# The last gate columns and the output projection move into the ordered list of the MLP, with pairs by seven products and rings of five

## The chip, the cores and the metric

The kernel runs on one core of a Trainium2 chip. The metric is device time in microseconds (us), the median of several executions. TensorE (PE) does the matmuls, VectorE (DVE) and ScalarE (ACT) the elementwise work, the sync engine (SP) issues the loads.

## The reference

Two layers of a hybrid decoder on x of 1 x 256 x 2048, float32:

```
h = rms_norm(x, attn_norm)
g_q, g_k, g_v, g_gate, g_lr, s_q, s_k, s_v = split(h @ w_in)           # 6160 columns
o_gla = rms_norm(gla_chunked(g_q, g_k, g_v, log_a), gla_out_norm) * silu(g_gate)   # 1024 columns
o_sb  = rms_norm(stick_breaking_attention(rms_norm(s_q), rms_norm(s_k), s_v), sb_out_norm)
x = x + concat(o_gla, o_sb) @ w_o                                      # 2048 x 2048
hm = rms_norm(x, mlp_norm)
x = x + square(relu(hm @ w_up)) @ w_down                               # 2048 x 8192, 8192 x 2048
```

## The kernel before

Every matmul operand is split into a high part and a low rest: ScalarE copies a raw weight tile to `whi`, VectorE subtracts to get `wlo`, and each product is three matmuls (high by `whi`, high by `wlo`, low by `whi`), 128x512 each. A *piece* is one `whi` and one `wlo` tile of 1024 columns; mostly 12 matmuls read it.

**Up to the output projection** the work goes in units of 512 columns (`unit`, L537, weights by `weight_parts`, L512). A scheduler orders the engines; `after(n, fn)` (L341) holds other work until n ticks later. The last two input units (L1051) give the 1024 gate columns in two halves. Of each half ScalarE makes a scaled copy (L1056) and then absolute value, exponential and logarithm (L1058 to L1060), VectorE takes the minimum (L1061), ScalarE the exponential (L1062), VectorE the product (L1063). `gated` (L1040) multiplies the attention results `on` by it, and TensorE turns them into `mixed`, the operand of the output projection. That has four units of 512 columns (L1078), each followed by `residual` (L1074), one addition of 128x1024 into x (`xb`), and by `norm_operand`, which turns `xb` into the MLP's operand `hm`.

**The MLP** is an ordered list (`Plan`, L40) of entries with an engine, a length, what they need, and a due time counted back from TensorE's order. `Plan.run` (L68) walks through them, taking for VectorE and ScalarE what is due first of what is ready in its own reckoning; the order that comes out is kept on PE, DVE and ACT (L1448), behind all that was issued before. The list has units of 1024 columns: for each quarter q two up units and two down units. The contraction of a unit runs over eight *pairs* of 128-row blocks, each with a raw tile of 1 MB. Five pairs take 8 products of 128x512; pairs 1, 3 and 5 (`fast`, L398) take 7 by Strassen's scheme (in Winograd's form): VectorE then makes sums of the weights (`ts`, `t`, L1195 on) and of the operand (`forms`, L401), and the seven results gather in seven PSUM banks (`m1` to `m7`; `m8` takes part in the plain pairs). `down_tail` (L1266) and `up_tail` (L1313) put the banks together, with 12 additions of 128x512 after each unit. `whi` and `wlo` have four buffers each (`RING`), raw tiles five (`RAWS`). The list starts with four entries of TensorE that stand for the work still under way (L1111).

Of the kernel before, what the change touches and what calls it, by code (L numbers as in the profile page):

```python
# [126 lines left out]
def trunk_kernel(  # L127
# [61 lines left out]
    MLP = ("sxh", "sx", "ts", "t4", "raw2")  # L189
# [544 lines left out]
    def norm_pair(po):  # L734

        o = tmp("on", [P, 512], bufs=4)
# [39 lines left out]
    for l in range(DEPTH):  # L776
# [234 lines left out]
        def gla_out(e, v, vc, S, sc):  # L1011
# [21 lines left out]
            ons[e] = norm_pair(po)  # L1033
# [6 lines left out]
        def gated(e, gate, c):  # L1040
            o = ons[e]
            o4 = o.rearrange("p (h t d) -> p h t d", h=2, t=NT)
            for tt in range(NT):
                nc.vector.tensor_tensor(
                    o4[:, :, tt, :], o4[:, :, tt, :],
                    gate[:, tt, c : c + 2 * P].rearrange("p (h d) -> p h d", d=P), ALU.mult,
                )
            after(1, lambda: to_operand(mixed, e, o, gain("gla", l)))

        for g in range(2):  # L1050
            ug = unit(hT, wl, 0, C_GG + g * 512, 512)  # L1051
            gate = act_tile(F32, (P, NT, 512))

            def gate_part(tt, ug, gate):
                gx = gate[:, tt, :]
                nc.scalar.activation(gx, ug[:, tt, :], AF.Copy, scale=rst[:, tt : tt + 1])  # L1056
                e = tmp("t2", [P, 512], bufs=4)
                nc.scalar.activation(e, gx, AF.Abs)  # L1058
                nc.scalar.activation(e, e, AF.Exp, scale=-1.0)
                nc.scalar.activation(e, e, AF.Ln, bias=1.0)  # L1060
                nc.vector.scalar_tensor_tensor(e, gx, 0.0, e, ALU.min, ALU.subtract)  # L1061
                nc.scalar.activation(e, e, AF.Exp)  # L1062
                nc.vector.tensor_tensor(gx, gx, e, ALU.mult)  # L1063
# [24 lines left out]

        mlp_psum()
        hT = Operand()  # L1090
# [4 lines left out]
        RING, RAWS = 4, 5  # L1095
# [7 lines left out]
        units = [(q, down, n2) for q in range(4) for down in range(2) for n2 in range(2)]  # L1103
# [13 lines left out]
        def norm_last():  # L1117

            sq = add("ACT", 2 * A1, lambda: norm_squares(3, ssq), x3)
            return norm_end(sq, ssq)  # L1120
# [22 lines left out]
        def weights(u, j):  # L1143
            q, down, n2 = units[u]
            if down:
                r0, c0, w = q * 2048, n2 * 1024, w_down[l]
            else:
                r0, c0, w = 0, q * 2048 + n2 * 1024, w_up[l]
            r0 += 2 * j * P
            return w[r0 : r0 + 2 * P, c0 : c0 + 1024].rearrange("(k p) n -> p k n", p=P)  # L1150

        def load(x):
# [15 lines left out]
        def parts(src, readers, deps, n=2):  # L1168
# [3 lines left out]

            def high():
                box["h"] = ppool.tile([P, 2, 512], F32R, tag="whi", name=nm("whi"), bufs=RING)
                nc.scalar.activation(box["h"][:, :n], src(), AF.Copy)  # L1175

            def low():
                box["l"] = ppool.tile([P, 2, 512], F32R, tag="wlo", name=nm("wlo"), bufs=RING)
# [16 lines left out]
        def steps(x, r, ld, readers):  # L1195

            u, j = divmod(x, 8)
            q, down, n2 = units[u]
            op = up[q] if down else hm
# [290 lines left out]
```

## Time and profile before

| | us |
|---|---|
| median of 3 runs | 2199.61 (2199.44 to 2200.23) |
| the profiled execution | 2201.5 |
| its span | 2199.8 |
| TensorE busy | 2187.7 |
| VectorE busy | 1790.0 |
| ScalarE busy | 1259.7 |

TensorE is the engine that is nearly always busy. A busy span counts a matmul from its start to its modelled end, and neighbours overlap; the pace is read from one start to the next. "Idle before" in a row names what ended the wait.

### The profile page before, as it was taken

The page shows a single profiled execution, that of the slowest core. Times are in us where ns is not written, and L with a number is a line of the kernel's source. Part 1 is how long each engine was busy: PE and PEld are TensorE (multiplying, and loading weights), DVE is VectorE, ACT ScalarE, POOL GpSimd, SP SyncE. Part 2 cuts the span into 40 slices and gives each one's busy share as a digit, 9 for nine tenths or more (in the row PEclk, how much of TensorE's full clock was granted, in tenths as well). Part 3 has the DMA queues.
Part 4 walks back from the last instruction along what each step waited for, and adds up shares of the span by engine and source line. Part 5 has one row for each costly group of instructions (what it writes and reads, how often), then busy time and mean ns, then how long its engine had stood idle before and what let it go on. Part 6 is the DMA issues. An engine that isn't in the chain of part 4 may idle for free.

```text
span 2199.8 us, 27163 instructions
## 1 busy us (share of the span) xinstructions
PE 2187.7 (99%) x10376; PEld 1806.0 (82%) x10376; DVE 1790.0 (81%) x2286; ACT 1259.7 (57%) x1623; POOL 38.0 (2%) x64
## 2 busy tenths in 40 slices
PE   9999999999999999999999999999999999999999
PEld 7988778888888888888888887788888888888887
DVE  5677556789999999999957775667999899999998
ACT  5555345566566566466656553555665655665663
POOL 0020000000000000000000200000000000000000
PEclk9999999999999999999999999999999999999999
DMA  6654446556556556655546544465656665565564
GB/s 223 199 157 154 153 154 220 165 195 208 193 196 203 189 192 198 216 180 198 165 156 192 172 154 152 140 242 172 201 182 198 199 207 195 195 203 183 194 202 140
DMA packets 152550, 408.97 MB, mean 186 GB/s; under 512 B 6650, under 2 KB 31810, under 8 KB 152420
## 3 DMA queue, kind: packets, MB, share of 16 engines
q1 hardware_dynamic: 152420, 407.24, 56.3%
q8 instruction: 81, 1.33, 0.3%
q14 instruction: 49, 0.40, 0.1%
HBM read 405.12 MB, written 2.10 MB: 185 GB/s over the span
## 4 chain that ended last, share of the span: by engine, by line
PE 90%; DVE 7%; issue 1%; ACT 1%; DMA 0%; SPq 0%; POOL 0%; ACTq 0%
PE acc L549 9%; PE acc L551 9%; PE acc L550 9%; DVE wlo L1179 3%; PE acc L596 3%; PE acc L600 1%; DVE ts L1098 1%; DVE act L426 1%; PE ps L1017 1%; PE ps L1029 1%; ACT whi L1175 1%; PE ps L441 0%; PE ps L976 0%; PE ps L712 0%; DVE sx L426 0%
## 5 line engine op out<-in xcount | busy, mean ns | idle before, releaser
L1175 ACT ACTIVATE whi<-raw 128x1024 fp32r<-128x1024 f32 x512 | 532.5, 1057 | 280.4 <-DVE xb L1098 22.2
L1179 DVE TENSOR_TENSOR wlo<-raw,whi 128x1024 fp32r<-128x1024 f32 x512 | 618.5, 1217 | 56.8 <-ACT whi L1175 52.9
L532 DVE TENSOR_TENSOR wlo<-raw,whi 128x1024 fp32r<-128x1024 f32 (+2 forms) x274 | 317.3, 1164 | 194.3 <-ACT whi L530 193.8
L530 ACT ACTIVATE whi<-raw 128x1024 fp32r<-128x1024 f32 (+2 forms) x274 | 273.7, 1005 | 295.4 <-PE acc L551 246.9
L549 PE MATMUL acc<-whi,act 128*128 128x512 f32 (+2 forms) x960 | 368.9, 384 | 0.8 <-ACT act L451 0.8
L550 PE MATMUL acc<-wlo,act 128*128 128x512 f32 (+2 forms) x960 | 362.4, 377 | 0.0
L551 PE MATMUL acc<-whi,act 128*128 128x512 f32 (+2 forms) x960 | 362.2, 377 | 0.0
L549 PEld LDWEIGHTS acc<-whi,act 128*128 128x128 f32 x960 | 181.3, 189 | 35.9 <-issue 4.1
L551 PEld LDWEIGHTS acc<-whi,act 128*128 128x128 f32 x960 | 180.9, 188 | 34.1 <-issue 0.7
L550 PEld LDWEIGHTS acc<-wlo,act 128*128 128x128 f32 x960 | 181.3, 189 | 31.1 <-issue 0.7
L1175 ACT ACTIVATE whi<-ts 128x1024 fp32r<-128x1024 f32 x96 | 101.5, 1057 | 103.0 <-PE m__1438_7186 L1260 3.9
L1179 DVE TENSOR_TENSOR wlo<-ts,whi 128x1024 fp32r<-128x1024 f32 x96 | 117.3, 1222 | 51.6 <-ACT whi L1175 51.6
L1175 ACT ACTIVATE whi<-t 128x512 fp32r<-128x512 f32 x96 | 60.6, 631 | 122.2 <-DVE t L1098 60.7
L1098 DVE TENSOR_TENSOR ts<-raw 128x1024 f32<-128x1024 f32 x96 | 117.1, 1220 | 1.2
L596 PE MATMUL acc<-act,whi 128*128 128x512 f32 x256 | 91.9, 402 | 0.0
L600 PE MATMUL acc<-act,wlo 128*128 128x256 f32 x256 | 71.8, 280 | 0.0
L1179 DVE TENSOR_TENSOR wlo<-t,whi 128x512 fp32r<-128x512 f32 x96 | 65.5, 682 | 1.6 <-ACT whi L1175 1.5
L1098 DVE TENSOR_TENSOR raw<-ts,raw 128x512 f32<-128x512 f32 x96 | 65.5, 683 | 0.4
L1098 DVE TENSOR_TENSOR t<-raw 128x512 f32<-128x512 f32 x96 | 65.5, 682 | 0.0
L1344 ACT ACTIVATE act<-act,st 128x512 f32<-128x512 f32 x64 | 46.1, 720 | 26.3 <-DVE act L1098 25.4
L596 PEld LDWEIGHTS acc<-act,whi 128*128 128x128 f32 x256 | 48.1, 188 | 11.1
L600 PEld LDWEIGHTS acc<-act,wlo 128*128 128x128 f32 x256 | 48.4, 189 | 0.1
(2401 smaller groups left out, 4585.1 us busy)
## 6 DMA issues: line engine op xcount, KB each, us to landing
raw<-in_w_up_dram SPq DMA_DIRECT2D x128, 1024.0 KB, 5.1
raw<-in_w_down_dram SPq DMA_DIRECT2D x128, 1024.0 KB, 5.3
raw<-in_w_in_dram SPq DMA_DIRECT2D x84, 1024.0 KB, 5.1
raw<-in_w_o_dram SPq DMA_DIRECT2D x32, 1024.0 KB, 5.1
raw<-in_w_in_dram SPq DMA_DIRECT2D x14, 512.0 KB, 6.6
raw<-in_w_in_dram SPq DMA_DIRECT2D x8, 544.0 KB, 3.8
out_dram<-xb SPq DMA_DIRECT2D x8, 256.0 KB, 2.0
xb<-in_x_dram SPq DMA_DIRECT2D x3, 512.0 KB, 8.2
```

The lines of the kernel that those rows point to most:

```text
L426: nc.vector.tensor_tensor(d[:, :, 1, :], src, f32(d[:, :, 0, :]), ALU.subtract)
L530: newest["hi"] = nc.scalar.activation(h, r, AF.Copy).ins
L532: newest["lo"] = nc.vector.tensor_tensor(lo[:, q : q + step, :width], r, f32(h), ALU.subtract).ins
L549: nc.tensor.matmul(o, xh[:, sl], whi[:, j, :width], start=first, stop=False)
L550: nc.tensor.matmul(o, xh[:, sl], wlo[:, j, :width], start=False, stop=False)
L551: st["mm"] = nc.tensor.matmul(o, xl[:, sl], whi[:, j, :width], start=False, stop=last).ins
L596: nc.tensor.matmul(acc[:, f, :], whi[:, j, sl], op.both(k), start=(k == 0), stop=False, skip_group_check=True,)
L600: nc.tensor.matmul(acc[:, f, T:], wlo[:, j, sl], xh, start=False, stop=(k == KT - 1), skip_group_check=True,)
L1098: nc.vector.tensor_tensor(dst, a, b, op)
L1175: nc.scalar.activation(box["h"][:, :n], src(), AF.Copy)
L1179: nc.vector.tensor_tensor(box["l"][:, :n], src(), f32(box["h"][:, :n]), ALU.subtract)
L1344: nc.scalar.activation(box[h][:, tt, :], box[h][:, tt, :], AF.Relu, scale=rr[:, tt : tt + 1],)
```

## The change

The second half of the gate columns becomes the first unit ("g") of the ordered list, and the output projection its next two ("o"), with 1024 columns each. The gate's arithmetic becomes entries of the list (`gate`), for the first half as well, whose copies are still issued ahead of the list. In an o unit pairs 0 and 1 go by seven products, in the order given by `pair_order`, and the results are added to x by `down_tail`. `whi` and `wlo` get a fifth buffer (`whi5`, `wlo5`), raw tiles go from five to four. The attention's buffers give way to the MLP's (`open_scope`) before the second gate unit instead of after the first projection unit.

```diff
-    MLP = ("sxh", "sx", "ts", "t4", "raw2")
+    MLP = ("whi5", "wlo5", "sxh", "sx", "ts", "t4", "raw2")
...
+    def norm_pair(po, o=None):
+
+        o = tmp("on", [P, 512], bufs=4) if o is None else o
...
-            ons[e] = norm_pair(po)
+            if e % 2 == 0:
+                ons["t", e // 2] = act_tile(F32, (P, 2, 512))
+            ons[e] = norm_pair(po, ons["t", e // 2][:, e % 2, :])
...
-        def gated(e, gate, c):
-            o = ons[e]
...
-            after(1, lambda: to_operand(mixed, e, o, gain("gla", l)))
-
-        for g in range(2):
-            ug = unit(hT, wl, 0, C_GG + g * 512, 512)
-            gate = act_tile(F32, (P, NT, 512))
...
-            gate_part(0, ug, gate)
-            after(1, lambda a=ug, b=gate: gate_part(1, a, b))
-            for hp in range(2):
-                after(3 + hp, lambda e=2 * g + hp, t=gate, c=hp * 2 * P: gated(e, t, c))
...
+        ug = unit(hT, wl, 0, C_GG, 512)
+        gates_t = [act_tile(F32, (P, NT, 512))]
+        for tt in range(NT):
+            nc.scalar.activation(
+                gates_t[0][:, tt, :], ug[:, tt, :], AF.Copy, scale=rst[:, tt : tt + 1]
+            )
+        assert not held
...
+        open_scope("sbuf", mlp=1)
         hm = Operand()
         ssq = new_ssq()
...
-        def residual(n, acc):
-            nc.vector.tensor_tensor(xb[n], acc, xb[n], ALU.add)
-
-        for n in range(4):
-            uo = unit(mixed, w_o[l], 0, n * 512, 512, (2, 3, 0, 1))
-            if n == 0:
-
-                open_scope("sbuf", mlp=1)
-            if n < 3:
-                residual(n, uo)
-                after(1, lambda n=n: norm_operand(hm, n, "mlp", l, sums=True))
-                after(2, lambda n=n: norm_squares(n, ssq))
-        assert not held
-
-
...
-        RING, RAWS = 4, 5
+        RING, RAWS = 5, 4
...
-        units = [(q, down, n2) for q in range(4) for down in range(2) for n2 in range(2)]
+
+        units = [("g", 0, 0), ("o", 0, 0), ("o", 0, 1)]
+        units += [(k, q, n2) for q in range(4) for k in ("up", "down") for n2 in range(2)]
+
+        def pair_order(u):
+
+            if units[u][0] != "o":
+                return range(8), {j for j in range(8) if fast(j)}
+            if units[u][2] == 0:
+                return (4, 5, 6, 7, 0, 1, 2, 3), {0, 1}
+            return (4, 5, 6, 0, 7, 1, 2, 3), {0, 1}
...
-        tail = [add("PE", 12 * MM, None) for _ in range(RING)]
-        for t in tail:
-            whi.append([t])
-            wlo.append([t])
-        x3 = add("DVE", V2, lambda: residual(3, uo), tail)
...
+        for _ in range(RING):
+            p = add("PE", 12 * MM, None)
+            whi.append([p])
+            wlo.append([p])
...
-        def turned(n, h2, m, op, key, ll, deps):
-
-            turn, high, low, _ = operand_parts(op, n, h2, key, ll, lambda: bank(m))
-            a = add("PE", 8 * TR / 2, turn, deps, free.get(m))
...
+        def turned(n, h2, m, op, key, ll, sums=False):
+
+            turn, high, low, scaled = operand_parts(op, n, h2, key, ll, lambda: bank(m))
+            i = 2 * n + h2
+            a = add("PE", 4 * TR, turn, x_done[n], free[m])
+            if sums and fast(i):
+                box = []
+                b = add("ACT", A1, lambda: box.append(scaled()), a)
+                free[m] = [b]
+                return made(lambda: forms(op, i, box[0], "sxh"), None, True, b)
...
             box = []
+            x = len(raws)
 
             def fn():
-                if x % 5 < 2:
-                    box.append(tmp("raw2", [P, 2, 1024], bufs=2))
+                if x % 4 == 0:
+                    box.append(tmp("raw2", [P, 2, 1024], bufs=1))
                 else:
                     box.append(wpool.tile([P, 2, 1024], F32, tag="raw", name=nm("raw")))
-                nc.sync.dma_start(box[0], weights(*divmod(x, 8)))
...
+            def part(tag):
+                if i % RING == 0:
+                    return tmp(tag + "5", [P, 2, 512], F32R, bufs=1)
+                return ppool.tile([P, 2, 512], F32R, tag=tag, name=nm(tag), bufs=RING - 1)
+
             def high():
-                box["h"] = ppool.tile([P, 2, 512], F32R, tag="whi", name=nm("whi"), bufs=RING)
+                box["h"] = part("whi")
                 nc.scalar.activation(box["h"][:, :n], src(), AF.Copy)
...
+            kind, q, _ = units[u]
+            op = {"g": hT_now, "o": mixed, "up": hm, "down": up.get(q)}[kind]
...
+            if kind == "g":
+                for s in range(2):
+                    yield parts(
+                        lambda s=s: r()[:, s, :].rearrange("p (c n) -> p c n", c=2),
+                        readers, ld,
+                    ), [(m, [(blk(k, tt, 2 * j + s), k) for k in range(2)])
+                        for tt, m in enumerate((1, 6))]
+                return
...
-            if not fast(j):
+            if not is_fast:
...
+        def gate(g):
+
+            y = gates_t[g]
...
+                def logs(gx=gx, box=box):
+                    box.append(tmp("t2", [P, 512], bufs=4))
+                    nc.scalar.activation(box[0], gx(), AF.Abs)
+                    nc.scalar.activation(box[0], box[0], AF.Exp, scale=-1.0)
+                    nc.scalar.activation(box[0], box[0], AF.Ln, bias=1.0)
...
+                a = add("ACT", 3 * A1, logs, gate_done.get((g, tt)))
+                b = add("DVE", V1, least, a)
+                c = add(
+                    "ACT", A1,
+                    lambda box=box: nc.scalar.activation(box[0], box[0], AF.Exp), b,
+                )
+                ends.append(add("DVE", V1, lambda gx=gx, box=box: combine(gx(), gx(), box[0], ALU.mult), c))
...
+                a = add("DVE", 0.7, gated, ends)
+                turns.append((g, 4 * TR, turn, a, m, e, high, low, scaled, box))
+
+        def turn_gated():
+
+            g, cost, turn, a, m, e, high, low, scaled, box = turns.pop(0)
+            p = add("PE", cost, turn, a, free[m])
+            if e < 2:
+                b = add("ACT", A1, scaled, p)
+                free[m] = [b]
+                done["o", 0, e] = made(lambda: forms(mixed, e, box[1], "sx"), None, True, b)
+            else:
+                b = add("ACT", A1, high, p)
+                done["o", 0, e] = add("DVE", 0.7, low, b)
+                free[m] = [b, done["o", 0, e]]
+
...
+            for tt, m in enumerate((1, 6)):
+                free[m] = [gate_done.get((1, 0))]
+                gate_done[1, tt] = add("ACT", A1, lambda a=(tt, m): copy(*a), p[m], free[m])
+                free[m] = [gate_done[1, tt]]
+            gate(1)
...
-        lastf = max(j for j in range(8) if fast(j))
+        hT_now, hT = hT, Operand()
         rr = rr_done = None
...
+        gate_done, turns, tails = {}, [], {}
+        gate(0)
+        for u, (kind, q, n2) in enumerate(units):
+            order, quick = pair_order(u)
+            if kind != "g":
+                tails[u] = (up_tail if kind == "up" else down_tail)(u)
...
+            lasts = [j for j in order if j in quick][-1]
+            for j in range(4) if kind == "g" else order:
+                final = j == (3 if kind == "g" else order[-1])
+                r, ld, readers = load(u, j)
+                for (box, h, lo), prods in steps(u, j, j in quick, r, ld, readers):
...
-                    if u == 0 and k == 0:
+                    was = units[u - 1] if u else None
+                    if kind == "g" and k == 4 or kind == "o" and n2 == 0 and k == 5:
+                        turn_gated()
+                        turn_gated()
+                    if k < 2 and was and was[0] == "up":
+                        tails[u - 1][2](k)
+                    if k < 2 and was == ("o", 0, 0) or was == ("o", 0, 1) and k < 2:
+                        n = 2 * was[2] + k
                         for h2 in range(2):
-                            done["hm", 6 + h2] = turned(
-                                3, h2, (5, 7)[h2], hm, "mlp", l, x3
+                            done["up", 0, 2 * n + h2] = turned(
+                                n, h2, ((5, 7), (1, 6))[k][h2], hm, "mlp", l, sums=True
                             )
...
-                if j == lastf:
+                if j == lasts and kind != "g":
                     tails[u][0](p)
+            if kind == "g":
+                g_tail(p)
+            if kind == "o" and n2 == 1:
+                rr, rr_done = norm_end([squares(n, ssq) for n in range(4)], ssq)
```

What the built order makes of it is seen best where the first gate unit ends, in the first layer (the second has the same). ScalarE before: `whi` are the tiles of the second gate unit, `act_2724` the scaled copy of the first one's result, `t` the scratch of its logarithms.

```order
L530 ACTIVATE whi_2736<-raw_2734 128x1024
L530 ACTIVATE whi_2760<-raw_2734 128x1024
L737 ACTIVATE on_2672<-ps_2661 128x512
L364 ACTIVATE st_2679<-st_2678 128x4
L365 ACTIVATE st_2679<-st_2679 128x4
L530 ACTIVATE whi_2778<-raw_2776 128x1024
L1056 ACTIVATE act_2724<-acc_2487,st_444 128x512 x2
L1058 ACTIVATE t_507_2726<-act_2724 128x512
L1058 ACTIVATE t_512_2753<-act_2724 128x512
L1059 ACTIVATE t_507_2726<-t_507_2726 128x512
L1059 ACTIVATE t_512_2753<-t_512_2753 128x512
L1060 ACTIVATE t_507_2726<-t_507_2726 128x512
```

ScalarE now, at the same place: `act_2722` is the copy, `whi_534_2782` the first tile of the second gate unit.

```order
L365 ACTIVATE st_2677<-st_2677 128x4
L1045 ACTIVATE act_2722<-acc_2486,st_444 128x512 x2
L1418 ACTIVATE t_529_2758<-act_2722 128x512
L1419 ACTIVATE t_529_2758<-t_529_2758 128x512
L1420 ACTIVATE t_529_2758<-t_529_2758 128x512
L1418 ACTIVATE t_531_2764<-act_2722 128x512
L1419 ACTIVATE t_531_2764<-t_531_2764 128x512
L1420 ACTIVATE t_531_2764<-t_531_2764 128x512
L1431 ACTIVATE t_529_2758<-t_529_2758 128x512
L1431 ACTIVATE t_531_2764<-t_531_2764 128x512
L1183 ACTIVATE whi_534_2782<-raw_530_2762 128x1024
L1183 ACTIVATE whi_2784<-raw_530_2762 128x1024
```

Three `whi` tiles of the next unit stood ahead of the copy, and none does now; all of the first half's eight functions stand ahead of the first.

VectorE before, at the same place: `wlo` are the rests of the second gate unit's tiles.

```order
L532 TENSOR_TENSOR wlo_2737<-raw_2734,whi_2736 128x1024
L532 TENSOR_TENSOR wlo_2761<-raw_2734,whi_2760 128x1024
...
L532 TENSOR_TENSOR wlo_2779<-raw_2776,whi_2778 128x1024
L1061 SCALAR_TENSOR_TENSOR t_507_2726<-act_2724,t_507_2726 128x512
L1061 SCALAR_TENSOR_TENSOR t_512_2753<-act_2724,t_512_2753 128x512
L532 TENSOR_TENSOR wlo_2797<-raw_2776,whi_2796 128x1024
L1063 TENSOR_TENSOR act_2724<-act_2724,t_507_2726 128x512
L1063 TENSOR_TENSOR act_2724<-act_2724,t_512_2753 128x512
L1044 TENSOR_TENSOR on_2332<-on_2332,act_2724 128x2x128 x2
```

VectorE now, at the same place.

```order
L623 TENSOR_TENSOR act_2571<-act_2571,st_2680 128x512
L1423 SCALAR_TENSOR_TENSOR t_529_2758<-act_2722,t_529_2758 128x512
L1423 SCALAR_TENSOR_TENSOR t_531_2764<-act_2722,t_531_2764 128x512
L1063 TENSOR_TENSOR act_2722<-act_2722,t_529_2758 128x512
L1063 TENSOR_TENSOR act_2722<-act_2722,t_531_2764 128x512
L1441 TENSOR_TENSOR act_2332<-act_2332,act_2722 128x2x128 x4
L1187 TENSOR_TENSOR wlo_536_2786<-raw_530_2762,whi_534_2782 128x1024
L1187 TENSOR_TENSOR wlo_2790<-raw_530_2762,whi_2784 128x1024
```

The first `wlo` of the second gate unit now comes behind the minimum, the product and the four slices of the gating (L1441); three came ahead of them.

## Rows read from the trace of the kernel before

**Rows 1.** The page: busy time, share of the span and instructions of each engine.

```profile
PE 2187.7 (99%) x10376; PEld 1806.0 (82%) x10376; DVE 1790.0 (81%) x2286; ACT 1259.7 (57%) x1623; POOL 38.0 (2%) x64
```

**Rows 2.** TensorE in order of time (start, length), first layer's second up unit.

```profile
482.19 0.39 PE L1258 MATMUL m__784_4104<-whi,act 128*128 128x512 f32 x1
...
483.55 0.39 PE L1258 MATMUL m__756_3993<-whi,act 128*128 128x512 f32 x1
484.36 0.50 PE L1259 MATMUL m__756_3993<-wlo,act 128*128 128x512 f32 x1 [0.42 <-DVE wlo L1179]
```

**Rows 3.** TensorE's waits (total us, times, longest), first and last of eleven.

```profile
PE m__756_3993 L1259 <- DVE wlo L1179: 0.4, 1, 0.4
...
PE m__659_3599 L1259 <- DVE wlo L1179: 0.3, 1, 0.3
```

**Rows 4.** Busy time by engine, granted clock, DMA: gate and projection; one MLP quarter.

```profile
330.00:419.00 89.00, 89.00 (x410) 73.91 (x409) 56.65 (x70) 48.48 (x71) 0.00 (x0) 1.00 0.62 210
462.00:633.00 171.00, 170.58 (x767) 140.58 (x766) 157.24 (x188) 102.63 (x120) 0.00 (x0) 1.00 0.60 197
```

**Rows 5.** TensorE in order of time where the first gate unit ends.

```profile
304.55 0.39 PE L551 MATMUL acc<-whi,act 128*128 128x512 f32 x1
304.77 0.39 PE L549 MATMUL acc<-whi,act 128*128 128x512 f32 x1
```

**Rows 6.** ScalarE in order of time at the same place; x2 merges two.

```profile
301.60 0.20 ACT L364 ACTIVATE st<-st 128x4 f32<-128x4 f32 x1 [1.68 <-DVE st L361]
301.83 0.20 ACT L365 ACTIVATE st<-st 128x4 f32<-128x4 f32 x1
302.25 1.06 ACT L530 ACTIVATE whi<-raw 128x1024 fp32r<-128x1024 f32 x1 [0.21 <-PE acc L551]
304.97 1.27 ACT L1056 ACTIVATE act<-acc,st 128x512 f32<-128x512 f32 x2 [1.66 <-PE acc L551]
306.13 1.15 ACT L1058 ACTIVATE t<-act 128x512 f32<-128x512 f32 x2
...
309.25 1.05 ACT L530 ACTIVATE whi<-raw 128x1024 fp32r<-128x1024 f32 x1
```

**Rows 7.** ScalarE by shape, 290 to 345 us (busy us, mean ns of one).

```profile
L1058 ACT ACTIVATE t<-act 128x512 f32<-128x512 f32 x4 | 2.3, 630 | 0.0
```

**Rows 8.** VectorE by shape, the same stretch.

```profile
L532 DVE TENSOR_TENSOR wlo<-raw,whi 128x1024 fp32r<-128x1024 f32 x18 | 21.5, 1222 | 7.9 <-ACT whi L530 7.7
...
L1061 DVE SCALAR_TENSOR_TENSOR t<-act,t 128x512 f32<-128x512 f32 x4 | 2.6, 688 | 8.7 <-ACT t L1060 8.7
L1063 DVE TENSOR_TENSOR act<-act,t 128x512 f32<-128x512 f32 x4 | 2.6, 686 | 0.0
```

**Rows 9.** VectorE in order of time: the gating of the first half.

```profile
312.69 1.43 DVE L1044 TENSOR_TENSOR on<-on,act 128x256 f32<-128x256 f32 x4
```

**Rows 10.** The sync queue in order of time: two loads together.

```profile
293.11 5.97 SPq L519 DMA_DIRECT2D raw<-in_w_in_dram  x2
```

**Rows 11.** The end of the run; columns as in rows 4.

```profile
2195.00:2196.00 1.00, 0.97 (x5) 0.47 (x3) 0.34 (x1) 0.00 (x0) 0.00 (x0) 1.00 0.58 217
2198.00:2199.00 1.00, 0.00 (x0) 0.00 (x0) 0.00 (x0) 0.00 (x0) 0.00 (x0) 0.53 0.25 94
```

**Rows 12.** TensorE in order of time: the first stream of the run.

```profile
9.47 0.63 PE L550 MATMUL acc<-wlo,act 128*128 128x512 f32 x1
9.90 0.66 PE L551 MATMUL acc<-whi,act 128*128 128x512 f32 x1
...
13.34 0.48 PE L550 MATMUL acc<-wlo,act 128*128 128x512 f32 x1
13.66 0.40 PE L551 MATMUL acc<-whi,act 128*128 128x512 f32 x1
```

**Rows 13.** VectorE by shape, 462 to 633 us.

```profile
L1179 DVE TENSOR_TENSOR wlo<-raw,whi 128x1024 fp32r<-128x1024 f32 x64 | 77.2, 1217 | 6.4 <-ACT whi L1175 5.9
...
L1098 DVE TENSOR_TENSOR t<-raw 128x512 f32<-128x512 f32 x12 | 8.2, 682 | 0.0
```

More of the change, by code (lines that the diff above doesn't have):

```diff
@@ L1108, in trunk_kernel, with squares @@
         x_done = {}
[L1111 to L1120 removed]
+        for _ in range(RING):
+            p = add("PE", 12 * MM, None)
+            whi.append([p])
+            wlo.append([p])
+        def squares(n, ss):
+            return add("ACT", 2 * A1, lambda: norm_squares(n, ss), x_done[n])
         def norm_end(sq, ss):
@@ L1132, in norm_end, with made, part @@
             return rr, add("DVE", 0.4, step, b)
-        def turned(n, h2, m, op, key, ll, deps):
-            turn, high, low, _ = operand_parts(op, n, h2, key, ll, lambda: bank(m))
-            a = add("PE", 8 * TR / 2, turn, deps, free.get(m))
+        def made(f, got, tag_fast, first):
+            box = []
+            def part(k):
+                if not box:
+                    box.extend(f())
+                box[k]()
+            e = first
+            if tag_fast:
+                e = add("DVE", 1.25, lambda: part(0), first)
+            b = add("ACT", A1 * (2 if tag_fast else 1), lambda: part(1), e)
+            return add("DVE", 1.1 if tag_fast else V1, lambda: part(2), b)
+        def turned(n, h2, m, op, key, ll, sums=False):
[3 more added lines that the diff above has]
+            if sums and fast(i):
+                box = []
+                b = add("ACT", A1, lambda: box.append(scaled()), a)
+                free[m] = [b]
+                return made(lambda: forms(op, i, box[0], "sxh"), None, True, b)
             b = add("ACT", A1, high, a)
@@ L1266, in down_tail @@
         def down_tail(u):
-            q, _, n2 = units[u]
-            end = q == 3 and l + 1 == DEPTH
+            kind, q, n2 = units[u]
+            end = kind == "down" and q == 3 and l + 1 == DEPTH
             x11, x21, x12, x22 = (
@@ L1351, in turn @@
             def turn(h):
-                q, _, n2 = units[u]
+                _, q, n2 = units[u]
                 op = up.setdefault(q, Operand())
@@ L1382, in turn @@
                     pair = 4 * n2 + 2 * h + i
-                    def made(k, box=box, h=h, i=i, pair=pair):
-                        key = "f", h, i
-                        if key not in box:
-                            box[key] = forms(op, pair, box["t", h][:, i], "sx")
-                        box[key][k]()
-                    e = sq
-                    if fast(pair):
-                        e = add("DVE", 1.25, lambda f=made: f(0), sq)
-                    b = add("ACT", A1 * (2 if fast(pair) else 1), lambda f=made: f(1), e)
@@ new lines, in g_tail, with copy @@
+        def g_tail(p):
+            gates_t.append(None)
+            def copy(tt, m):
+                if tt == 0:
+                    gates_t[1] = act_tile(F32, (P, NT, 512))
+                nc.scalar.activation(
+                    gates_t[1][:, tt, :], banks[m], AF.Copy, scale=rst[:, tt : tt + 1]
+                )
+            for tt, m in enumerate((1, 6)):
[3 more added lines that the diff above has]
+            gate(1)
@@ L1401, in trunk_kernel @@
         for m in (5, 7, 1, 6, 2, 4, 3, 8):
             free[m] = []
-        lastf = max(j for j in range(8) if fast(j))
+        hT_now, hT = hT, Operand()
         rr = rr_done = None
-        tails = {}
-        for u, (q, down, n2) in enumerate(units):
-            tails[u] = (down_tail if down else up_tail)(u)
-            begun, p, k = set(), {}, 0
-            for j in range(8):
-                x = 8 * u + j
-                r, ld, readers = load(x)
-                for (box, h, lo), prods in steps(x, r, ld, readers):
-                    ready = done.get((q, j) if down else ("hm", j))
-                    for m, blocks in prods:
-                        begin, end = m not in begun, j == (7 if m in (2, 4, 3, 8) else lastf)
+        gate_done, turns, tails = {}, [], {}
@@ new lines, in trunk_kernel @@
+        gate(0)
[3 more added lines that the diff above has]
+                tails[u] = (up_tail if kind == "up" else down_tail)(u)
+            begun, p, k = set(), {}, 0
+            lasts = [j for j in order if j in quick][-1]
[3 more added lines that the diff above has]
+                for (box, h, lo), prods in steps(u, j, j in quick, r, ld, readers):
+                    ready = done.get((kind, q, j))
+                    for m, blocks in prods:
+                        begin = m not in begun
+                        if kind == "g":
+                            end = final and k == 7
+                        else:
+                            end = final if m in (2, 4, 3, 8) else j == lasts
```

114 lines of the change are left out of this document (67 added, 47 removed).

## The prediction, made before the changed kernel had run

> **What bounds the kernel now.** I read the busy time per engine first: TensorE is busy for 2187.7 of 2199.8 us, 99% [rows 1]. So time can come from two things alone: fewer or shorter matmuls, or gaps opened and closed on TensorE. One 128x512 matmul costs the pitch at which they start: six of them stand between 482.19 and 483.55, 0.227 us each [rows 2]. The 0.39 of a single row is its length in the pipe and is not the price.
>
> Then the gaps. In the ordered list TensorE waits eleven times, each time for a `wlo` tile of VectorE [rows 3]. At 484.36 the second matmul of a piece starts 0.81 after the first, so 0.58 is lost [rows 2]. I take 0.55 for each of nine such seams, and 0.48 for the two in the first up unit of a layer, whose waits are a tenth shorter (0.3 against 0.4 [rows 3]). VectorE is what is late there: it is busy for 157.24 of 171 us in the MLP, but only for 56.65 of 89 in the stage from the second gate unit through the output projection [rows 4]. The reader is to see that the projection has slack on VectorE and the MLP has almost none.
>
> Last, how the end of a gate unit looks now. TensorE's last matmul of the unit starts at 304.55 and the next unit's first at 304.77, without a gap [rows 5]. ScalarE begins the two copies of the result at 304.97 [rows 6]; meanwhile TensorE lives on tiles that ScalarE made earlier, such as the one at 302.25. In the order before, three `whi` tiles of the next unit stand ahead of the copies.
>
> **The change part by part.**
>
> *Products.* In each of two projection units per layer two pairs take 7 products in place of 8, three matmuls each: 2 x 2 x 2 x 3 = 24 matmuls, 24 x 0.227 = **5.4 us saved**. The transposes move but stay as many, and so do the loads: 4 for the second gate unit and 16 for the projection, 1 MB each.
>
> *The new start of the list.* This is the costly part. The list now begins with the second gate unit, and its order puts all the logs and exponentials of the first gate (8 activations) ahead of the first `whi` tile. They read the copies, and those wait for the last matmul of the unit before. ScalarE issues in order: at 306.13 and 309.25 the rows come as the program has them [rows 6]. So when that last matmul ends no piece of the next unit exists, and TensorE stands still until ScalarE and then VectorE have got through. With 0 for the start of the copies (304.97 in the trace of before): two copies take 1.16, until the row at 306.13 [rows 6]. Independent 128x512 activations start 0.52 apart (1.15 for two less 0.63) and one that needs the one before waits for its end: 0.63 [rows 7] and 0.03, as from 301.60 to 301.83 with a length of 0.20 [rows 6]. Absolute value, exponential and logarithm of the first half thus start at 1.16, 1.81 and 2.46, those of the second at 2.98, 3.63 and 4.28, the last exponential of the first half at 4.80. That of the second half waits for VectorE's minimum, 0.69 [rows 8] after 4.91, and starts at 5.69. The first `whi` starts at 6.21 and takes 1.06: TensorE can issue one matmul at about 7.3. The second one needs `wlo`, which in VectorE's order stands behind the second half's product (0.69, ends 7.05) and the gating of four slices at 0.36 (1.43 for four [rows 9]). It starts near 8.35, takes 1.22 [rows 8], and the second matmul goes at 9.6. At the present pace it would have gone at 0.03. **9.6 us lost per layer, 19.3 in all** (before rounding). Bounds: were no activation to wait for the one before, 8.8; with 0.1 for each such wait and no overlap of neighbours, 10.5. What is queued behind: on ScalarE all further `whi`, on VectorE all further `wlo`, and on the sync queue the loads that reuse their tiles; none of these ends later than TensorE needs it, since a piece takes TensorE 12 x 0.227 = 2.72 and the two engines 1.06 and 1.22.
>
> The load of the gate's first tile is no part of that. It stands behind three other loads on the sync queue and waits for the last `wlo` of the unit before, whose counterpart issues with another at 293.11 [rows 10]; both of those are over by 299.1, some 6 us ahead of the copies.
>
> *The restart.* After the idle stretch the matmuls may start at the slow level. At the end of the run TensorE's last matmul ends at 2195.97, and in 2198 to 2199 the granted clock averages 0.53 [rows 11]: it went to half, 1.2 GHz, within about 2.1 us of idling. In the first stream of the run, matmuls from 9.47 to 13.34 stand 0.43 apart (nine intervals) and then go over to the faster pitch [rows 12], though the clock column there shows no change. Nine at 0.20 too much, and the one in transition, give about **2.0 us per restart, 4.0 in all**; bounds 0 (the clock stays) and 2.2 each.
>
> The Trainium skill, "TensorE: Matmul & The Clock Gate", Part 1, says the slow state is the default and activity releases it, so that an idle gap in mid-kernel is paid again afterwards. That speaks against this change: by it the 4.0 stand in the sum, and by the clock column of the first 13 us alone they would not; the end of the run agrees with the page. The same page's table of specs says that ScalarE and VectorE take their queues strictly in order, and that only TensorE reorders. Were that false, the opposite rival below would hold.
>
> *Rings of five.* With four tiles TensorE's need overtakes VectorE by 0.5 at the seams. A fifth puts one more piece in store (2.72, or some 1.2 in a pair by sevens), more than is missing: nine seams at 0.55, **5.0 saved**; bounds 0 and 5.0. One raw buffer fewer costs nothing: a buffer is loaded three pairs, some 15 us, ahead, against 6 for two loads issued together [rows 10].
>
> *VectorE in the projection.* A unit now has 12 additions of 0.60 where two of 1.14 stood, and each fast pair four more passes. By pitches (1.14 and 0.60, the lengths of [rows 13] less their overlap) the second projection unit asks about 40 us of VectorE against 44 of TensorE (186 matmuls and 16 transposes at 0.11). It fits, so I cost it at nothing inside the unit. But the store is drained when the first up unit begins: from the end of the last product VectorE has, by the order's rows and these pitches, 22.3 us of work up to the `wlo` of the fifth pair, with about 0.9 of waits for transposes, and TensorE wants it after 22.4. That is 1.0 late per layer where 0.48 is lost now: **1.0 more in all**; bounds 0 and 3.
>
> Sum: -5.4 + 19.3 + 4.0 - 5.0 + 1.0 = +13.9. The profiled execution took 2201.5, so its like would take 2215.4; it lies 1.9 above the median of the runs, 2199.61, and on the median the forecast is **2213.5 us**, 0.6% slower.
>
> **The rivals.** (a) *The clock holds* through the gaps: 4.0 less, 2209.5. For it: one lone matmul at 7.3 splits the gap; against: the first part is still longer than 2.1. (b) *The ring doesn't help*, because VectorE itself is short of time at the seams, not of store: nine stalls stay and the projection's additions add a few more tenths, 2219. For it: 157.24 of 171 [rows 4]; against: the missing amount is only about half a microsecond. (c) *The second gate's chain is late too.* Its copies can start only when the second gate unit ends, and its transposes stand in TensorE's order 16 us later; ten activations and four `whi` between them take about 10. If it were 3 late per layer: 2219.5. (d) *Faster:* the first `whi` doesn't wait for the first gate, so the start of the list is covered as the unit border at 304.77 is now [rows 5]. Then 19.3 and 4.0 fall away: 2190. The point that decides: the stall and restart together must stay under 4.7 per layer ((5.4 + 5.0 - 1.0) / 2), and the eight activations, two copies and one `whi` alone take ScalarE more than 6. (e) *The change cancels out:* a stall and restart of some 5 per layer leave 2200. It needs half of the chain to have been done before the unit ends, and nothing in the order allows that.
>
> **How the numbers follow.** Forecast 0.62; (a) 0.10; (b) 0.13; (c) 0.06; (d) 0.05; (e) 0.04. Within 0.2%, 4.4 us, a measurement of this kernel can't tell a time from no change. Cases on the slow side add up to 0.91, (e) to 0.04, (d) to 0.05. The range reaches over (a) and to (b), with the bounds of the stall (8.8 to 10.5) and of the restart: 2207 to 2220; (d), (e) and the tails of (b) and (c) are left out.
>
> **What would show it.** At the end of the first gate unit, in each layer, TensorE waits about 7.4 us for the ScalarE tile `whi5`, issues one matmul, waits some 2.3 for `wlo5`, then starts matmuls 0.43 apart for about 4 us, with a granted clock under 1 there. The eleven waits for `wlo` in the list shrink to two. The 128x512 matmuls are 24 fewer. The forecast is wrong if TensorE has no gap of over 5 us, if VectorE's waits grow inside the projection, or if the seams keep their 0.55.

## The result, and the profile after

The changed kernel takes **2209.32 us** (median of 5 runs, 2208.87 to 2210.54) against 2199.61 before: ratio 1.0044, 95% interval 1.003 to 1.0059. It is 0.4% slower. The forecast was 2213.5, 0.6% slower, with a range of 2207 to 2220. The profiled execution took 2209.32 as well, with a span of 2207.6.

The page's row of busy times, to be held against [rows 1]:

```profile
PE 2180.8 (99%) x10352; PEld 1805.5 (82%) x10352; DVE 1851.7 (84%) x2386; ACT 1276.5 (58%) x1651; POOL 38.0 (2%) x64
```

TensorE has 24 instructions fewer and is busy 6.9 us less, yet the span is 7.8 longer. So it waits more. Its waits, from the largest down (total us, times, longest):

```profile
PE m__510_2737 L1274 <- ACT whi L1183: 7.4, 1, 7.4
PE m__2403_11911 L1274 <- ACT whi L1183: 7.4, 1, 7.4
...
PE m__510_2737 L1275 <- DVE wlo L1187: 1.5, 1, 1.5
PE m__2403_11911 L1275 <- DVE wlo L1187: 1.5, 1, 1.5
...
PE m__715_3698 L1275 <- DVE wlo L1187: 0.4, 1, 0.4
PE m__1855_9038 L1275 <- DVE wlo L1187: 0.4, 1, 0.4
...
PE m__2602_12866 L1275 <- DVE wlo L1187: 0.4, 1, 0.4
```

Four new waits, two per layer, and of the eleven short ones of [rows 3] three. The place of the new ones, where the first gate unit ends in the first layer, on TensorE in order of time:

```profile
303.07 0.39 PE L551 MATMUL acc<-whi,act 128*128 128x512 f32 x1
310.90 0.79 PE L1274 MATMUL m__510_2737<-whi,act 128*128 128x512 f32 x1 [7.44 <-ACT whi L1183]
313.16 0.80 PE L1275 MATMUL m__510_2737<-wlo,act 128*128 128x512 f32 x1 [1.47 <-DVE wlo L1187]
313.75 0.63 PE L1276 MATMUL m__510_2737<-whi,act 128*128 128x512 f32 x1
314.18 0.63 PE L1274 MATMUL m__510_2737<-whi,act 128*128 128x512 f32 x1
...
318.87 0.48 PE L1276 MATMUL m__510_2737<-whi,act 128*128 128x512 f32 x1
319.19 0.39 PE L1274 MATMUL m__510_2737<-whi,act 128*128 128x512 f32 x1
```

At the pace of 0.227 the second matmul of the g unit would have started 0.45 after 303.07; it starts 10.09 after, 9.63 late. Then the matmuls start 0.43 apart up to 318.87. ScalarE and VectorE at the same place:

```profile
303.56 1.27 ACT L1045 ACTIVATE act<-acc,st 128x512 f32<-128x512 f32 x2 [2.99 <-PE acc L551]
304.72 0.63 ACT L1418 ACTIVATE t<-act 128x512 f32<-128x512 f32 x1
...
309.27 0.63 ACT L1431 ACTIVATE t<-t 128x512 f32<-128x512 f32 x1 [0.24 <-DVE t L1423]
309.81 4.83 ACT L1183 ACTIVATE whi<-raw 128x1024 fp32r<-128x1024 f32 x5
```

```profile
310.54 1.43 DVE L1441 TENSOR_TENSOR act<-act,act 128x256 f32<-128x256 f32 x4
311.88 3.49 DVE L1187 TENSOR_TENSOR wlo<-raw,whi 128x1024 fp32r<-128x1024 f32 x3
```

Counted from the copies at 303.56, the first function starts at 1.16, the last at 5.71, the first `whi` at 6.25 and the first `wlo` at 8.32. The forecast had 1.16, 5.69, 6.21 and 8.35. The clock, by stretches (columns as in [rows 4]), first and second layer:

```profile
303.00:310.90 7.90, 0.46 (x3) 0.04 (x1) 2.95 (x6) 6.97 (x12) 0.00 (x0) 0.65 0.00 1
310.90:313.10 2.20, 0.79 (x1) 0.29 (x1) 2.20 (x6) 2.20 (x3) 0.00 (x0) 0.50 0.00 0
313.10:319.30 6.20, 6.14 (x15) 4.85 (x16) 4.55 (x5) 2.58 (x3) 0.00 (x0) 0.52 0.59 188
319.30:330.00 10.70, 10.70 (x52) 8.88 (x51) 4.91 (x4) 3.58 (x5) 0.00 (x0) 1.00 0.72 245
...
1411.30:1415.20 3.90, 3.83 (x10) 3.08 (x11) 3.90 (x5) 1.55 (x2) 0.00 (x0) 0.56 0.41 96
1415.20:1425.00 9.80, 9.80 (x45) 8.11 (x44) 4.33 (x4) 4.25 (x4) 0.00 (x0) 1.00 0.81 291
```

The granted clock is 0.50, 1.2 GHz, after the gap, and 1.00 again from 319.3 and 1415.2.

**Where the time went, by stages.** I took four stages from the starts of the same matmuls in every trace: the run up to the first matmul of L658 (the attention); the *border*, from the last matmul of L1029 (24 matmuls before the first gate unit ends) to the second gate unit's first; *gate and projection*, from there to the first up unit's first; the *MLP*, from there to the next layer's first matmul of L549, or in the second layer to the last matmul of the run. In the first layer the last three stages begin and end at 299.00, 304.77, 418.26 and 1105.53 in the kernel before, and at 297.53, 310.90, 425.50 and 1109.29 in the changed one (the table is rounded from nanoseconds). The attention (234.0 to 234.1) and the second layer's start (52.45) are alike in all. First and second layer, us:

| kernel | run up to L658 | border | gate and projection | MLP |
|---|---|---|---|---|
| before | 64.98 | 5.77, 5.77 | 113.49, 113.49 | 687.27, 684.33 |
| changed | 63.47 | 13.38, 13.38 | 114.60, 113.41 | 683.79, 680.88 |
| ring_five_alone | 63.28 | 5.77, 5.78 | 113.49, 113.49 | 681.64, 678.85 |
| first_gate_behind | 64.95 | 5.77, 5.78 | 109.68, 109.68 | 683.71, 680.87 |
| gap_filled | 64.23 | 14.84, 14.84 | 110.40, 110.40 | 683.70, 680.86 |
| o_by_eight | 62.47 | 13.37, 13.37 | 116.17, 116.38 | 682.55, 679.76 |
| functions_behind | 63.58 | 7.35, 7.35 | 109.83, 109.83 | 683.75, 681.15 |
| first_up_reordered | 64.67 | 5.77, 5.77 | 109.68, 109.68 | 683.35, 680.51 |
| change_with_ring_four | 64.34 | 13.37, 13.37 | 114.59, 114.15 | 688.93, 685.93 |
| raw_four_alone | 65.06 | 5.77, 5.77 | 113.49, 113.49 | 687.03, 684.22 |

The change loses 15.2 at the borders and 1.0 in gate and projection, and gains 6.9 in the MLP: +9.3. The profiled executions differ by less, 7.8, since the one of before began 1.5 slower; that stage varies from 62.5 to 65.1 over the ten profiled executions, whose code is the same up to there, with the number of slow matmuls in the first stream [rows 12]: at most 2 intervals of 0.43 in the four executions up to 63.6, 8 to 10 in the others.

### The profile page after: what moved, and what is told of

Read it like the earlier page. It is cut to its first block, busy times and chain, and to the rows that moved or that the text cites. A ratio compares the mean times of both kernels' runs of the same rounds, so it can differ in the third digit from the quotient of the medians.

```text
span 2207.6 us, 27192 instructions
## 1 busy us (share of the span) xinstructions
PE 2180.8 (99%) x10352; PEld 1805.5 (82%) x10352; DVE 1851.7 (84%) x2386; ACT 1276.5 (58%) x1651; POOL 38.0 (2%) x64
## 3 DMA queue, kind: packets, MB, share of 16 engines
q8 instruction: 81, 1.33, 0.2%
## 4 chain that ended last, share of the span: by engine, by line
PE 97%; DVE 1%; ACT 1%; issue 0%; DMA 0%; SPq 0%; POOL 0%; ACTq 0%
PE acc L549 6%; PE acc L550 6%; PE acc L551 6%; PE acc L596 3%; PE acc L600 1%; PE ps L1017 1%; PE ps L1029 1%; DVE wlo L1187 0%; PE ps L976 0%; PE ps L712 0%; PE ps L658 0%; PE ps L676 0%; DMA raw<-in_w_in_dram 0%; PE m__510_2737 L1275 0%; PE m__2403_11911 L1275 0%
## 5 line engine op out<-in xcount | busy, mean ns | idle before, releaser
L1183 ACT ACTIVATE whi<-raw 128x1024 fp32r<-128x1024 f32 x592 | 616.2, 1058 | 364.8 <-ACT whi L1183 11.6
L1187 DVE TENSOR_TENSOR wlo<-raw,whi 128x1024 fp32r<-128x1024 f32 x592 | 716.7, 1220 | 105.1 <-ACT whi L1183 100.1
L532 DVE TENSOR_TENSOR wlo<-raw,whi 128x1024 fp32r<-128x1024 f32 (+2 forms) x194 | 220.5, 1140 | 133.0 <-ACT whi L530 132.8
L530 ACT ACTIVATE whi<-raw 128x1024 fp32r<-128x1024 f32 (+2 forms) x194 | 189.8, 983 | 205.4 <-PE acc L551 156.1
L549 PE MATMUL acc<-whi,act 128*128 128x512 f32 (+2 forms) x640 | 242.3, 379 | 0.7 <-ACT act L451 0.7
L550 PE MATMUL acc<-wlo,act 128*128 128x512 f32 (+2 forms) x640 | 237.5, 371 | 0.3 <-DVE wlo L532 0.3
L551 PE MATMUL acc<-whi,act 128*128 128x512 f32 (+2 forms) x640 | 237.1, 371 | 0.0
L549 PEld LDWEIGHTS acc<-whi,act 128*128 128x128 f32 x640 | 120.7, 189 | 23.6 <-issue 4.1
L551 PEld LDWEIGHTS acc<-whi,act 128*128 128x128 f32 x640 | 120.5, 188 | 21.2 <-issue 0.7
L550 PEld LDWEIGHTS acc<-wlo,act 128*128 128x128 f32 x640 | 120.7, 189 | 19.7 <-DVE wlo L532 1.0
L1187 DVE TENSOR_TENSOR wlo<-ts,whi 128x1024 fp32r<-128x1024 f32 x104 | 127.2, 1223 | 7.4 <-ACT whi L1183 6.3
L1063 DVE TENSOR_TENSOR ts<-raw 128x1024 f32<-128x1024 f32 x104 | 126.9, 1220 | 1.3
L596 PEld LDWEIGHTS acc<-act,whi 128*128 128x128 f32 x256 | 48.2, 188 | 11.1
```

The lines of the kernel that those rows point to most:

```text
L530: newest["hi"] = nc.scalar.activation(h, r, AF.Copy).ins
L532: newest["lo"] = nc.vector.tensor_tensor(lo[:, q : q + step, :width], r, f32(h), ALU.subtract).ins
L549: nc.tensor.matmul(o, xh[:, sl], whi[:, j, :width], start=first, stop=False)
L550: nc.tensor.matmul(o, xh[:, sl], wlo[:, j, :width], start=False, stop=False)
L551: st["mm"] = nc.tensor.matmul(o, xl[:, sl], whi[:, j, :width], start=False, stop=last).ins
L596: nc.tensor.matmul(acc[:, f, :], whi[:, j, sl], op.both(k), start=(k == 0), stop=False, skip_group_check=True,)
```

## The experiments

Each run's ratio is to the kernel before on the same chip, with its 95% interval.

**ring_five_alone.** The kernel before with the ring of the change.

```diff
-        RING, RAWS = 4, 5
+        RING, RAWS = 5, 4
...
+            def part(tag):
+                if i % RING == 0:
+                    return tmp(tag + "5", [P, 2, 512], F32R, bufs=1)
+                return ppool.tile([P, 2, 512], F32R, tag=tag, name=nm(tag), bufs=RING - 1)
...
```

> The kernel before (2199.6 us) with nothing but five buffers for whi and wlo in the ordered list and four raw tiles in place of five. Theory A, the forecast's term: nine seams of 0.55 go, -5.0, about 2194.6. Theory B, as the trace of the changed kernel is read: each large seam costs about 0.67 (two late rows, not one) and eight small seams of about 0.2 per layer go too, so -8 to -8.5, about 2191.4. Theory C, VectorE is short of time and not of store, or the raw tile that is missing costs what the ring gives: 2199.6, no gain.

2188.83 us (2188.11 to 2190.67), ratio 0.9947 (0.9935 to 0.996). By stages the MLP is 5.63 and 5.48 shorter, 11.1 in all, and nothing else moves. That is more than A and B said. Theory C falls. What the ring removes is seen in rows of the kernel before that the forecast did not count, TensorE in order of time:

```profile
484.70 0.40 PE L1260 MATMUL m__756_3993<-whi,act 128*128 128x512 f32 x1
...
558.88 0.39 PE L1258 MATMUL m__917_4739<-whi,act 128*128 128x512 f32 x1
559.18 0.50 PE L1259 MATMUL m__917_4739<-wlo,act 128*128 128x512 f32 x1
559.52 0.39 PE L1260 MATMUL m__917_4739<-whi,act 128*128 128x512 f32 x1
```

The row behind each late one is late too: 484.70 follows 484.36 [rows 2] by 0.34, not 0.227. And at 559.18 a matmul starts 0.07 late without any idle time marked, because the one before is still counted as busy (0.39 long at a pace of 0.227), and the next 0.11 late. Fourteen such small seams, from this one to 2164.96, stand in the MLP of before; with the ring of five there is none, and of the eleven waits one is left, at the end of the first layer's MLP.

**raw_four_alone.** The kernel before with four raw tiles and its ring of four, `RING, RAWS = 4, 4`.

> The kernel before with four raw tiles in place of five and its ring of four. Theory A: the loads come early enough, no change against the kernel before (within 1 us), and all that the run with the ring alone gained is the ring's. Theory B: each pair waits for its load now and then: 2 us slower or more, and the ring is worth that much more.

2200.58 us (2199.24 to 2201.29), ratio 1.0002 (0.9993 to 1.0011). Theory A holds: the raw tile costs nothing (by stages the MLP is even 0.24 and 0.11 shorter), and what ring_five_alone gains is the ring's.

**change_with_ring_four.** The changed kernel with `RING, RAWS = 4, 5` and all ring tiles from one pool.

> The changed kernel with four buffers for whi and wlo and five raw tiles, as before the change. Theory A, the forecast's term for the seams: 5 us slower than the changed kernel. Theory B, by the run with the ring alone: 11 to 12 slower.

2219.59 us (2217.43 to 2221.14), ratio 1.0088 (1.0074 to 1.0102), about 10 above the changed kernel. The MLP is 5.14 and 5.05 longer. This is near B: beside the other edits the ring is worth 10.2.

**first_gate_behind.** The copies of the first half become an entry of the list, due behind the first whi tiles, and the g unit goes to banks that they don't read.

```diff
+        def first_copies():
+            for tt in range(NT):
+                nc.scalar.activation(
+                    gates_t[0][:, tt, :], ug[:, tt, :], AF.Copy, scale=rst[:, tt : tt + 1]
+                )
+            mlp_psum()
+
+        gate_done[0, 0] = gate_done[0, 1] = add("ACT", 2 * A1, first_copies, whi[RING - 2])
         gate(0)
...
-                        for tt, m in enumerate((1, 6))]
+                        for tt, m in enumerate((5, 7))]
...
-                m = (5, 7)[hp]
+                m = (1, 6)[hp]
...
-            for tt, m in enumerate((1, 6)):
+            for tt, m in enumerate((5, 7)):
```

> The changed kernel (2209.3 us) with the copies and functions of the first gate half entered into the ordered list behind its first three whi tiles, and the g unit in two banks that the copies don't read. Theory A: the wait at the end of the first gate unit comes from ScalarE's order alone; stall (2 x 9.6) and restart (2.8 and 1.6) go, and nothing else becomes late: 2209.3 - 23.7 = 2185.6. Theory B, the gate's chain is needed early anyway: the transposes of the gated pairs now come late in the g unit and 3 us or more per layer are lost there: 2191 or above. Theory C, the loads of the first raw tiles are what is late, and the functions only stood before them: 2205 to 2209.

2186.86 us (2184.52 to 2186.98), ratio 0.9933 (0.9919 to 0.9946). Theory A. TensorE and ScalarE at the border, in order of time:

```profile
304.60 0.39 PE L551 MATMUL acc<-whi,act 128*128 128x512 f32 x1
304.82 0.39 PE L1269 MATMUL m__530_2768<-whi,act 128*128 128x512 f32 x1
```

```profile
302.00 2.94 ACT L1178 ACTIVATE whi<-raw 128x1024 fp32r<-128x1024 f32 x3
305.08 1.27 ACT L1511 ACTIVATE act<-acc,st 128x512 f32<-128x512 f32 x2
```

The same products, loads and functions, and no gap: what the border cost was the order on ScalarE, and on VectorE behind it. Against this run the changed kernel loses 7.6 per layer at the border and 4.92 and 3.73 in gate and projection, of which 2.03 each is the wait for the first `wlo`. The rest, 2.89 and 1.70, is the restart; the lateness of the slow matmuls of the changed kernel, added up from start to start, gives the same two numbers.

**functions_behind.** One line alone, in the changed kernel.

```diff
+        gate_done[0, 0] = gate_done[0, 1] = whi[RING - 2][0]
         gate(0)
```

> The changed kernel with one line more: the planner is told that the functions of the first gate half can begin only with the fourth of its five stand-ins for the unit before. They then stand behind the first whi tiles, and the two copies behind the first. The g unit still writes to banks that the copies read. Theory A: what cost 9.6 us per layer is the row of functions; only the copies are waited for now, 1.2 to 1.6 per layer, in a gap too short for the clock to fall: 2 to 3 us above the version with copies and functions behind, about 21 under the changed kernel. Theory B: the slow matmuls come with any wait at this place: another 4 us more, about 17 under the changed kernel. Theory C: the copies alone make the wait: a few us at most are gained.

2189.9 us (2188.26 to 2190.59), ratio 0.9953 (0.994 to 0.9965). Theory A: TensorE waits for the copies and for nothing else, 1.58 per layer at the border, and the matmuls behind go at the fast pace. The median lies 19.4 under the changed kernel, between A's 21 and B's 17; what decides for A is the clock of 1.00 in the rows. TensorE in order of time, and the busy time and clock of two stretches:

```profile
303.18 0.39 PE L551 MATMUL acc<-whi,act 128*128 128x512 f32 x1
304.99 0.50 PE L1274 MATMUL m__510_2737<-whi,act 128*128 128x512 f32 x1 [1.42 <-ACT act L1045]
305.32 0.39 PE L1275 MATMUL m__510_2737<-wlo,act 128*128 128x512 f32 x1
305.55 0.40 PE L1276 MATMUL m__510_2737<-whi,act 128*128 128x512 f32 x1
```

```profile
303.30:304.90 1.60, 0.27 (x2) 0.00 (x0) 0.00 (x0) 1.23 (x3) 0.00 (x0) 1.00 0.00 0
304.90:308.00 3.10, 3.02 (x13) 2.50 (x14) 2.09 (x2) 3.07 (x5) 0.00 (x0) 1.00 0.01 3
```

**gap_filled.** The gap in the changed kernel is filled with matmuls that nobody reads.

```diff
+        def filler():
+            o = bank(8)
+            for i in range(40):
+                nc.tensor.matmul(o, hT_now.t[0][:, 0, 0, :P], hT_now.both(1), start=True, stop=True)
+
+        add("PE", 0.0, filler)
```

> The changed kernel (2209.3 us) with 40 matmuls of 128x512 that nobody reads ahead of the first matmul of the g unit, in a bank that is free then; they take 40 x 0.227 = 9.1 us of the 9.6 that TensorE waits. Theory A, the slow matmuls after the gap come from the idle time: the clock stays high, the stall stays as long, and the restart is saved, 2.8 + 1.6 = 4.4: 2204.9. Theory B, the slow matmuls come from something else at the start of the list (operands, the new order, the loads): they stay, 2209.3 or a few tenths more.

2205.11 us (2204.31 to 2206.53), ratio 1.0021 (1.0012 to 1.0029). By stages, border and projection together are 2.73 and 1.55 shorter than in the changed kernel: Theory A, 4.28 against 4.4 expected. The slow matmuls came from the idle time. The clock in the gap and behind it:

```profile
303.50:313.90 10.40, 9.98 (x45) 7.92 (x43) 5.20 (x10) 9.25 (x14) 0.00 (x0) 1.00 0.00 1
313.90:318.00 4.10, 4.09 (x18) 3.40 (x19) 4.10 (x4) 2.55 (x3) 0.00 (x0) 1.00 0.40 113
```

**o_by_eight.** No pair of the projection goes by seven.

```diff
-                return (4, 5, 6, 7, 0, 1, 2, 3), {0, 1}
-            return (4, 5, 6, 0, 7, 1, 2, 3), {0, 1}
+                return (4, 5, 6, 7, 0, 1, 2, 3), set()
+            return (4, 5, 6, 0, 7, 1, 2, 3), set()
...
+            if kind == "o":
+                box["s"] = (None, None, None, None)
+
...
-            if e < 2:
+            if False:
...
```

> The changed kernel (2209.3 us) with all eight pairs of the two o units by eight products, in the same order of pairs, and the sums added to x in two passes for each half. Theory A, the forecast's term: 24 more matmuls, +5.4, and nothing for VectorE's additions: 2214.7. Theory B, the additions and sums for the fast pairs make VectorE late at the start of the first up unit, where the trace of the changed kernel has 1.3 us of waits in the second layer; without them 1 to 2.5 of the 5.4 come back: 2212 to 2213.7.

2213.06 us (2210.58 to 2214.36), ratio 1.0054 (1.0041 to 1.0066). By stages, gate and projection are 1.57 and 2.97 longer (the restarts, which differ from run to run, are in it: 1.74 and 1.95 here) and the MLP 1.24 and 1.12 shorter. Without the restarts the stage is 2.72 longer in each layer, which is the price of 12 matmuls. That is Theory B: 2.4 of the 5.4 that the products save are given back in the first up unit.

**first_up_reordered.** First_gate_behind with another order of pairs in the first up unit.

```diff
+            if u == 3:
+                return (0, 2, 1, 4, 3, 6, 5, 7), {j for j in range(8) if fast(j)}
```

> The version with copies and functions behind (2186.9 us), with the pairs of the first up unit in the order 0, 2, 1, 4, 3, 6, 5, 7 in place of 0 to 7: the pairs by seven, which take most of VectorE, come later. Theory A: the 1.3 us per layer that are lost in the first up unit against the kernel with the ring alone come from VectorE's store being drained by the projection's additions; two slow pairs let it fill: 2 to 2.6 us less, about 2184.5. Theory B: the loss is tied to the operand (the norm's last tiles come late), not to the order of the pairs: no change.

2184.74 us (2183.94 to 2185.83), ratio 0.9931 (0.9918 to 0.9943), the fastest of all, but the intervals of the two overlap. By stages the MLP is only 0.36 shorter per layer. TensorE's waits in the two first up units are gone, and one has come at the start of the second:

```profile
PE m__2684_13249 L1271 <- DVE act L1058: 0.5, 1, 0.5
PE m__797_4081 L1271 <- DVE act L1058: 0.5, 1, 0.5
```

L1058 there is the addition that puts the banks together. Pair 5, by seven, is now the last but one, so its banks come free late. The store was what lacked, as Theory A says: about 1.2 per layer is gained inside the first up unit, and some 0.8 of it is given back where the second begins. A's size, 2 to 2.6, is not confirmed: by stages the MLP gains 0.72 in all, and the rest of the distance between the two medians lies within their spread.

## Why the forecast was right, and which terms were off

| term | forecast | measured |
|---|---|---|
| products | -5.4 | -5.4 (24 fewer; 2 x 2.72 by o_by_eight) |
| stall at the border | +19.3 | +19.3 (2 x 9.63) |
| restart | +4.0 | +4.6 (2.89 and 1.70; filled: 2.73 and 1.55) |
| rings of five, outside the first up units | -5.0 | -9.9 |
| first up units, against before | +1.0 | +1.3 |
| inside gate and projection | 0 | -0.6 |
| sum | +13.9 | +9.3 (medians +9.7) |

The ring and the first up unit touch, so I split them as the forecast did, whose nine seams leave out the two first up units. A unit's lateness is its time from first matmul to first matmul, less 183 matmuls at the pace and its transposes at 0.10. The first up units are 0.71 and 0.74 late before, 0.10 each with the ring alone, 1.41 and 1.33 in the changed kernel, and 1.41 and 1.39 in change_with_ring_four. So 1.2 of the 11.1 that the ring gives alone is won in these units, and the changed kernel does not get it: there the ring is worth 10.2. Against ring_five_alone the changed kernel's MLP is 2.15 and 2.03 longer, of which 8 transposes per layer, which moved there from the projection, make 0.8 and are no loss; the other 2.6 is the 1.2 not won and the 1.3 of the table, to rounding. Inside gate and projection: 109.68 against 113.49 is 3.81 less, of which 12 matmuls make 2.72 and those transposes 0.8; what the other 0.3 per layer is was not traced.

**The stall** came as worked out, because every row of the chain stood in the trace of before and ScalarE took its queue in the order that the program has. That the functions, the copies and the load each could have been the cause was told apart: the load not at all (first_gate_behind has the same loads and no gap), the copies 1.58 per layer, the functions, with VectorE's part of the gate behind them, the other 8.

**The restart** was right in kind, with rival (a) refuted: the granted clock was at 0.50 before the lone matmul of 310.90 came, so that one had nothing to hold.

```profile
309.00:310.90 1.90, 0.00 (x0) 0.00 (x0) 1.80 (x5) 1.66 (x4) 0.00 (x0) 0.50 0.00 0
```

Its size was a little short: the first layer's 2.89 lies above the stated bound of 2.2, because 12 intervals were slow where the first stream of the run had nine. The page that the forecast weighed (the Trainium skill, "TensorE: Matmul & The Clock Gate", Part 1) says that a long wait in mid-kernel sends TensorE back to the slow level. The trace agrees: 0.50 and 0.43 apart after 7.4 us of waiting.

**The ring** is the term that was mis-sized, in the step "nine seams at 0.55, 5.0 saved; bounds 0 and 5.0". Measured outside the first up units it is 9.9, twice the bound. I listed seams by idle time and by starts that were late by more than half a microsecond. That left out the second late row of each seam and all seams under 0.2. Rival (b), that the ring would not help, was wrong; its condition, VectorE short of time, does not hold on the mean of a quarter (157.24 of 171 us [rows 4]). That one more tile in store is enough says that VectorE falls behind only for a few pieces in a row.

**The first up unit** was right in its mechanism (the store is drained by the projection's additions; o_by_eight takes the lateness down to 0.21 per layer) and near in its size, +1.3 against +1.0, though the working as written gives 0.8 late per layer (22.3 + 0.9 - 22.4) and not 1.0. The wait came at the fifth pair, as forecast:

```profile
448.20 0.39 PE L1274 MATMUL m__715_3698<-whi,act 128*128 128x512 f32 x1
448.97 0.51 PE L1275 MATMUL m__715_3698<-wlo,act 128*128 128x512 f32 x1 [0.38 <-DVE wlo L1187]
```

That is 0.66 with the row behind it. About 0.4 more stands at the third pair, up to 438.35, which the forecast didn't count. Of the eleven waits one more than the two expected is left, at 1088.28, as it was before.

**The sum.** The ring's error of -4.9 and +0.3 from the other terms left the forecast 4 too high; the range held it. Of the other rivals, (c) did not come: TensorE waits nowhere for the second gate's copies or transposes. What (d) described is what first_gate_behind brings about, 2186.9 where (d) said 2190. Against (e), stall and restart together were 12.5 and 11.3 per layer, not 5.

**What the kernel could have been:** by the table the change without its stall and restart is worth -14.6 (9.3 - 19.3 - 4.6), and first_gate_behind lies 14.2 under the kernel before. But the ring alone gives 11.1 of that. The move of gate and projection into the list with pairs by seven adds about 3.4 (2 x 3.81 less 2.15 and 2.03).

## What to carry to other kernels

When work is moved into a planned list, every input that comes from outside needs a stand-in with the time at which it will be there; one that has none counts as ready at the start, and an engine that takes its queue in order then waits for it with everything else behind. Count lateness from start to start over all instructions of a kind, not by the idle column: where operations overlap, small losses are not marked as idle, and here the rows without a marked wait made up half of what a deeper ring was worth. Several edits in one change should be timed alone too: the one worth 11 of 14 us was a line about buffers.

## What the runs showed of the hardware

A wait of 1.42 us on TensorE (functions_behind) left the granted clock at 1.00, and one of 7.44 (the changed kernel) took it to 0.50. After that gap the number of matmuls 0.43 apart was not the same in the two layers of one execution, 12 intervals up to 318.87 and 6 up to 1414.53, for the same instructions. So a restart has a price only as a range: the six of the three kernels with that gap cost 1.70 to 2.89 us.
